# A hybrid decoder layer with product-key experts: the second half's output product and norm in one pass of four blocks

## The chip, the cores and the metric

The kernel runs on one core of a Trainium2 chip. Its time is the device time of one execution in microseconds (us), and the median of several executions is compared. Five engines work side by side, each through its own queue of instructions: TensorE (PE, matrix products), VectorE (DVE), ScalarE (ACT), GpSimd (POOL) and SyncE (SP, which issues most DMA transfers). Semaphores order the engines among each other.

## The reference

One step of a one-layer decoder: 1024 prompt tokens and 8 sample tokens of width 1024. Three gated branches (dilated attention, a convolution, attention to a memory) are merged; what concerns this change comes after the merge:

```python
x1 = x + merged @ w_o
h2 = rms_norm(x1, g_norm2)
y  = x1 + peer(h2)

def peer(xb):                                   # for each token
    q = (xb @ w_pq).reshape(nb, 8, 2, 128)      # 8 heads, two halves of a key
    s = einsum('bhcd,ckd->bhck', q, sub_keys)   # 2 x 128 scores a head
    s1, i1 = top_k(s[:, :, 0], 16); s2, i2 = top_k(s[:, :, 1], 16)
    sc, ci = top_k(s1[..., :, None] + s2[..., None, :], 16)
    e = i1[ci // 16] * 128 + i2[ci % 16]        # 128 experts a token, of 16384
    g = softmax(sc)
    return einsum('be,bed->bd', g * gelu(xb . u_tab[e]), v_tab[e])
```

## The kernel before

All products are made in float32 precision from split operands: a weight or activation is cast to a shorter float on ACT (L158, L170), the residue is formed on DVE (L159, L171), and `mm3` (L173 to L176) issues three matmuls for one product. `load_w` (L161) loads 128 x 1024 values of a weight (512 KB) and splits them.

The 1024 prompt tokens are eight blocks of 128. The kernel goes through the first half (blocks 0 to 3, with the sample tokens as a fifth block) and then through the second (4 to 7). For a half, `front` makes the branches and the merged rows, and `tail` (L759) does the rest: the product with `w_o` into PSUM banks `po` (L775 to L789, eight `load_w` calls), the sum `x1`, its store to `x1scr`, the norm with `g_norm2` (`norm_rows`), the store of `h2` to `h2scr`, and its transposed split copy `h2h`, `h2l`. Then `topk` (L809) makes the queries (`pq`, 16 column groups of `w_pq`), the scores, and on DVE the selection: the best 16 of 128 twice (L847 to L851), the best 16 of their sums (`cand`, L862 to L876), one-hot lookups (L903 to L913), and the indices (`idxB`, L942, one of the last steps of a block that goes to the gathers).

The experts are worked off in two ways. Blocks 0 to 4 go the **dense** way: `gate_build` (L1016) makes gate matrices of all 16384 experts (products `pG`, stored to `gscr`), and `peer_dense` (L1063) goes over the expert table in 128 chunks `i1` of 128 experts: `pa` = scores of 640 tokens in two halves, gelu on ACT into `ge` (L1102), times the gate `Gt` on DVE (L1104), split into `hh` (L1107) and `hl` (L1108), and after each six chunks the products `pv` with `v_tab`, in two column halves, added into `dacc` (L1124). `uh`, `ul` are the split of a chunk of `u_tab`, `vh`, `vl` of `v_tab`. Chunks go through two `ge` buffers and three score banks. Blocks 5 to 7 go by **gathers**: `peer_gather` (L961) fetches for each of 128 slots a row of `u_tab` and `v_tab` for every token by an indirect DMA on POOL (L981), forms the dot product on DVE (L985) and adds the weighted row into `gacc` (L995). Half of the gather buffers (`uv0_2`, `uv0_3` and on) and the dense accumulator `dacc` lie in memory that the selection of the second half uses until its last step.

Before, the second half's tail runs twice: `tail("1a")` for blocks 4 and 5, with the gate build of block 4 behind it, and `tail("1b")` for blocks 6 and 7. In both, three PSUM banks serve the `po` and `pq` products.

A list scheduler fixes the order of each engine's queue when the kernel is built, from the priorities that stand in the code (`tc.cur_priority`); the gathers are given a lower priority than the work around them. On the chip a queue is worked off in that order.

Of the kernel before, what the change touches and what calls it, by code (L numbers as in the profile page):

```python
# [10 lines left out]
F32R = mybir.dt.float32r  # L11
# [10 lines left out]
P = 128  # L22
D = 1024
KD = D // P
# [22 lines left out]
def peer_trunk(tc, I, O):  # L47
# [11 lines left out]
    with contextlib.ExitStack() as es:  # L59
# [699 lines left out]
        def tail(tid, keep, wp, merged_h, merged_l, tblocks, after=None, kpool=None):  # L759
# [4 lines left out]
            with contextlib.ExitStack() as left:  # L764
                left.enter_context(banks(f"tail{tid}"))
                hp = left.enter_context(tc.tile_pool(name=f"h2t{tid}", bufs=1))
                with tc.tile_pool(name=f"tail{tid}", bufs=1) as tp:
# [7 lines left out]
                    for cg in range(2):  # L775
                        gs = slice(cg * 512, cg * 512 + 512)
                        pss = [mm_tile(f"po{tid}{cg}{c0}") for c0, _, _ in tblocks]
                        for kk in range(4):
                            wh, wl = load_w(wp, w_o[:, 2 * kk : 2 * kk + 2, gs], 2, 512, f"o{tid}{cg}{kk}")
                            for j in range(2):  # L780
                                k = 2 * kk + j
                                for bi, (c0, n, _) in enumerate(tblocks):
                                    sl = slice(c0, c0 + n)
                                    mm3(
                                        pss[bi][:n], merged_h[:, k, sl], merged_l[:, k, sl], wh[:, j], wl[:, j],
                                        k == 0, k == KD - 1,
                                    )
                        for bi, (c0, n, _) in enumerate(tblocks):
                            nc.vector.tensor_tensor(x1[bi][:n, gs], x1[bi][:n, gs], pss[bi][:n], op=OP.add)  # L789
                    if tid == "0":  # L790
                        h2h = keep.tile([P, KD, HALF + NS], F32R, tag="hTh", name=f"h2h{tid}")
                        h2l = keep.tile([P, KD, HALF + NS], F32R, tag="hTl", name=f"h2l{tid}")
                    else:
                        h2h = hp.tile([P, KD, TT], F32R, name=f"h2h{tid}")
                        h2l = hp.tile([P, KD, TT], F32R, name=f"h2l{tid}")
# [6 lines left out]
                with contextlib.ExitStack() as kes:  # L802
                    kp = kpool or kes.enter_context(tc.tile_pool(name="topk", bufs=1, side="right"))
                    topk(tid, kp, wp, h2h, h2l, [(c - m0, n, row) for c, n, row in tblocks], left, after)

        def topk(tid, kp, wp, h2h, h2l, tblocks, left, after):
            TT = sum(n for _, n, _ in tblocks)
            tchunks = [(0, TT)] if TT <= 512 else [(0, TT // 2), (TT // 2, TT // 2)]
            nb = len(tblocks)  # L809
            sv = kp.tile([P, nb, 16, TOPK], F32, name=f"sv{tid}")  # L810
            ix = kp.tile([P, nb, 16, TOPK], U32, name=f"ix{tid}")
            wx = left.enter_context(tc.tile_pool(name=f"wx{tid}", bufs=1)) if tid == "1a" else wp
            for hc in range(16):
# [3 lines left out]
                for c0, cn in tchunks:  # L817
                    cs = slice(c0, c0 + cn)
                    pq = mm_tile(f"pq{tid}{hc}{c0}")
                    for k in range(KD):  # L820
                        mm3(pq[:, :cn], wh[:, k], wl[:, k], h2h[:, k, cs], h2l[:, k, cs], k == 0, k == KD - 1)
# [306 lines left out]
        with tc.tile_pool(name="keep", bufs=1) as keep, tc.tile_pool(name="wts", bufs=1) as wp:  # L1128
# [3 lines left out]
            tail("0", keep, wp, *mg, [(b * P, P, b * P) for b in range(4)] + [(HALF, NS, SEQ)])  # L1132
            tc.cur_priority = p0
            phase.update(mm=3, o=1, g=2)
            with tc.tile_pool(name="psG", bufs=1, space=PSUM) as pgs:
# [11 lines left out]
                with (  # L1147
# [5 lines left out]
                    tail(  # L1153
                        "1a", keep, wp, *mg, [(b * P, P, HALF + b * P) for b in (0, 1)],
                        after=lambda b: gate_build(gb, pgs, (b * P, b * P + P), 8), kpool=kp,
                    )
                    tail("1b", keep, wp, *mg, [(b * P, P, HALF + b * P) for b in (2, 3)], kpool=kp)
# [88 lines left out]
```

## Time and profile before

| | |
|---|---|
| median of 3 runs | 3703.09 us (3703.05 to 3704.65) |
| profiled execution | 3695.24 us |
| its span | 3693.1 us |
| PE busy | 3429.9 us, 93% |
| DVE busy | 2899.1 us, 78% |
| ACT busy | 1499.6 us, 41% |
| POOL busy | 565.7 us, 15% |

The rows come from one profiled execution, whose own time stands beside its span. In a row of a window, "PE busy (x)" is the time in which the engine worked and how many instructions; PEld is the load of weights into PE; PEclk is the clock granted to PE as a share of full speed; then follow the mean busy share of the 16 DMA engines and what they moved. In a timeline a row begins with the start and the duration of an instruction (x3: three in a row), and what stands in brackets is the idle time before it and what ended it. A row of waits gives microseconds in total, their number, and the longest.

The stages along the span: memory and first front to about 655 us, first `w_o` pass and queries to 843, first selection to about 1007, gate build of blocks 0 to 3 with the second front to 1555, then the second half's tail to about 1897 with the dense pass beginning at 1828, and dense pass and gathers to the end.

### The profile page before, as it was taken

The page shows a single profiled execution, that of the slowest core. Times are in us where ns is not written, and L with a number is a line of the kernel's source. Part 1 is how long each engine was busy: PE and PEld are TensorE (multiplying, and loading weights), DVE is VectorE, ACT ScalarE, POOL GpSimd, SP SyncE. Part 2 cuts the span into 40 slices and gives each one's busy share as a digit, 9 for nine tenths or more (in the row PEclk, how much of TensorE's full clock was granted, in tenths as well). Part 3 has the DMA queues.
Part 4 walks back from the last instruction along what each step waited for, and adds up shares of the span by engine and source line. Part 5 has one row for each costly group of instructions (what it writes and reads, how often), then busy time and mean ns, then how long its engine had stood idle before and what let it go on. Part 6 is the DMA issues. An engine that isn't in the chain of part 4 may idle for free.

```text
span 3693.1 us, 55182 instructions
## 1 busy us (share of the span) xinstructions
PE 3429.9 (93%) x19969; PEld 3011.5 (82%) x19969; DVE 2899.1 (78%) x6275; ACT 1499.6 (41%) x3519; POOL 565.7 (15%) x398
## 2 busy tenths in 40 slices
PE   8987999898889989887899999999999999999998
PEld 6766989697677778676798888888989888898987
DVE  4358555499998656779988888887988888798988
ACT  6553552235755554344443333332333333233332
POOL 0000000000000000000012323322323332233332
PEclk9997999999999999998799999999999999999999
DMA  5467455423355546753668988888988988888987
GB/s 180 136 199 259 154 184 183 154 86 119 103 186 189 177 157 211 246 188 131 224 233 314 338 312 330 310 318 309 336 328 324 342 315 304 308 327 318 334 329 279
DMA packets 338454, 902.09 MB, mean 244 GB/s; under 512 B 32588, under 2 KB 140276, under 8 KB 285436
## 3 DMA queue, kind: packets, MB, share of 16 engines
q1 hardware_dynamic: 281732, 487.49, 39.7%
q0 software_dynamic: 56448, 411.07, 29.2%
q8 instruction: 157, 2.57, 0.3%
q14 instruction: 117, 0.96, 0.1%
HBM read 804.09 MB, written 94.83 MB: 243 GB/s over the span
## 4 chain that ended last, share of the span: by engine, by line
PE 31%; issue 30%; DVE 14%; DMA 13%; POOL 11%; ACT 2%; SPq 0%; POOLq 0%; DVEq 0%; ACTq 0%
POOL uv L981 11%; DMA uv<-in_uv,idxB 4%; PE pg L175 2%; PE pg L174 2%; PE pg L176 2%; PE pG L1057 2%; PE pG L1056 2%; DMA vr<-in_v_tab 1%; PE p_q L175 1%; PE p_q L176 1%; DMA wko<-kscr 1%; PE p_q L174 1%; DMA uv<-in_uv,idxS 1%; PE pa L174 1%; PE pa L176 1%
## 5 line engine op out<-in xcount | busy, mean ns | idle before, releaser
L981 POOL DMA_INDIRECT uv<-in_uv,idxB x384 | 555.8, 1448 | 1553.2 <-DVE gacc L995 1226.1
L174 PE MATMUL pa<-h2Ah,uh 128*128 128x320 f32 x2048 | 633.7, 310 | 2.2 <-ACT uh L158 2.2
L176 PE MATMUL pa<-h2Ah,ul 128*128 128x320 f32 x2048 | 631.9, 310 | 2.3 <-DVE ul L159 2.2
L175 PE MATMUL pa<-h2Al,uh 128*128 128x320 f32 x2048 | 633.2, 309 | 0.0
L985 DVE CUSTOM_DVE_ANT_0 uv<-uv,gh 128x1024 f32<-128x1024 f32 x392 | 478.5, 1222 | 138.2 <-DMA uv<-in_uv,idxB 119.9
L174 PE MATMUL pv<-vh,hh 128*128 128x512 f32 x1280 | 480.5, 396 | 44.3 <-ACT vh L158 28.4
L995 DVE SCALAR_TENSOR_TENSOR gacc<-uv,av,gacc 128x1024 f32<-128x1024 f32 x392 | 502.5, 1282 | 17.5 <-ACT av L993 12.6
L175 PE MATMUL pv<-vl,hh 128*128 128x512 f32 x1280 | 505.2, 395 | 9.3 <-DVE vl L159 9.3
L176 PE MATMUL pv<-vh,hl 128*128 128x512 f32 x1280 | 499.9, 393 | 0.0
L174 PEld LDWEIGHTS pa<-h2Ah,uh 128*128 128x128 f32 x2048 | 385.7, 188 | 6.9 <-ACT uh L158 2.4
L176 PEld LDWEIGHTS pa<-h2Ah,ul 128*128 128x128 f32 x2048 | 385.1, 188 | 5.4 <-DVE ul L159 2.8
L175 PEld LDWEIGHTS pa<-h2Al,uh 128*128 128x128 f32 x2048 | 385.4, 188 | 3.3 <-issue 0.9
L158 ACT CAST vh<-vr 128x512 fp32r<-128x512 f32 x256 | 157.2, 619 | 422.0 <-DMA vr<-in_v_tab 238.1
L174 PEld LDWEIGHTS pv<-vh,hh 128*128 128x128 f32 x1280 | 242.7, 190 | 99.0 <-ACT vh L158 40.0
L175 PEld LDWEIGHTS pv<-vl,hh 128*128 128x128 f32 x1280 | 243.6, 190 | 61.0 <-DVE vl L159 12.9
L176 PEld LDWEIGHTS pv<-vh,hl 128*128 128x128 f32 x1280 | 243.4, 190 | 50.0
L981 POOL DMA_INDIRECT uv<-in_uv,idxS x8 | 9.2, 1149 | 1556.3 <-ACT co L739 1513.2
L159 DVE TENSOR_TENSOR vl<-vr,vh 128x512 fp32r<-128x512 f32 x256 | 175.6, 688 | 77.0 <-ACT vh L158 76.5
L174 PE MATMUL pg<-hTh,wh_g 128*128 128x260 f32 (+1 forms) x576 | 192.9, 335 | 0.0
L175 PE MATMUL pg<-hTl,wh_g 128*128 128x260 f32 (+1 forms) x576 | 192.4, 334 | 0.0
L176 PE MATMUL pg<-hTh,wl_g 128*128 128x260 f32 (+1 forms) x576 | 192.3, 334 | 0.0
L990 ACT ACTIVATE av<-av 128x2 f32<-128x2 f32 x196 | 39.9, 204 | 375.3 <-DVE av L985 374.8
(558 smaller groups left out, 7651.3 us busy)
## 6 DMA issues: line engine op xcount, KB each, us to landing
ur<-in_uT SPq DMA_DIRECT2D x128, 512.0 KB
vr<-in_v_tab SPq DMA_DIRECT2D x256, 256.0 KB
gscr<-stg SPq DMA_DIRECT2D x20, 2048.0 KB
Gt<-gscr SPq DMA_DIRECT2D x32, 1280.0 KB
wr_g<-in_w_col SPq DMA_DIRECT2D x48, 512.0 KB
wr_q<-in_w_in SPq DMA_DIRECT2D x24, 512.0 KB
wr_u<-in_w_col SPq DMA_DIRECT2D x16, 512.0 KB
wr_pq<-in_w_col SPq DMA_DIRECT2D x16, 512.0 KB
```

The lines of the kernel that those rows point to most:

```text
L158: nc.scalar.copy(hi, raw)
L159: nc.vector.tensor_tensor(lo, raw, hi.bitcast(F32), op=OP.subtract)
L174: nc.tensor.matmul(out, ah, bh, start=start, stop=False)
L175: nc.tensor.matmul(out, ah, bl, start=False, stop=False)
L176: nc.tensor.matmul(out, al, bh, start=False, stop=stop)
L981: nc.gpsimd.indirect_dma_start(out=uv, out_offset=None, in_=I["uv"], in_offset=bass.IndirectOffsetOnAxis(ap=col, axis=0),)
L985: nc.vector.tensor_tensor_reduce(out=uv[:, 0:D], in0=uv[:, 0:D], in1=h2, scale=1.0, scalar=0.0, op0=OP.mult, op1=OP.add, accum_out=av[:, s ...
L990: nc.scalar.activation(av, av, AF.Gelu_apprx_tanh)
L995: nc.vector.scalar_tensor_tensor(acc, uv[:, D:], av[:, j : j + 1], acc, op0=OP.mult, op1=OP.add)
L1056: nc.tensor.matmul(pG[:, q], o2[:, a, :, q], wh[:, a, :, q], start=True, stop=False)
L1057: nc.tensor.matmul(pG[:, q], o2[:, a, :, q], wl[:, a, :, q], start=False, stop=True)
```

## The change

`tail` is called once for the second half, with all four blocks. The `po` product of the fourth block takes a bank of the transposes (`t_tile` slot 2), since there are three `mm` banks. `h2h` and `h2l` lie for both halves in `keep`, where they stood for the first half only. `topk` is called by a function that `tail` is given: for the second half twice, "1a" for blocks 4 and 5 (with the gate build of block 4 behind it) and "1b" for blocks 6 and 7. The product with `w_pq` reads its columns with the offset `m0`. So `w_o` is loaded, cast and split eight times for the second half instead of sixteen, and `g_norm2` once instead of twice.

```diff
-        def tail(tid, keep, wp, merged_h, merged_l, tblocks, after=None, kpool=None):
+        def tail(tid, keep, wp, merged_h, merged_l, tblocks, choose):
...
-                hp = left.enter_context(tc.tile_pool(name=f"h2t{tid}", bufs=1))
...
-                        pss = [mm_tile(f"po{tid}{cg}{c0}") for c0, _, _ in tblocks]
+                        pss = [
+                            mm_tile(f"po{tid}{cg}{c0}") if bi < phase["mm"] else t_tile(f"po{tid}{cg}{c0}", 2)
+                            for bi, (c0, _, _) in enumerate(tblocks)
+                        ]
...
-                    if tid == "0":
-                        h2h = keep.tile([P, KD, HALF + NS], F32R, tag="hTh", name=f"h2h{tid}")
-                        h2l = keep.tile([P, KD, HALF + NS], F32R, tag="hTl", name=f"h2l{tid}")
-                    else:
-                        h2h = hp.tile([P, KD, TT], F32R, name=f"h2h{tid}")
-                        h2l = hp.tile([P, KD, TT], F32R, name=f"h2l{tid}")
+                    h2h = keep.tile([P, KD, HALF + NS], F32R, tag="hTh", name=f"h2h{tid}")
+                    h2l = keep.tile([P, KD, HALF + NS], F32R, tag="hTl", name=f"h2l{tid}")
...
-                with contextlib.ExitStack() as kes:
-                    kp = kpool or kes.enter_context(tc.tile_pool(name="topk", bufs=1, side="right"))
-                    topk(tid, kp, wp, h2h, h2l, [(c - m0, n, row) for c, n, row in tblocks], left, after)
-
-        def topk(tid, kp, wp, h2h, h2l, tblocks, left, after):
+                choose(h2h, h2l)
+
+        def topk(tid, kp, wp, h2h, h2l, tblocks, after=None):
...
+            left = contextlib.ExitStack()
...
-                        mm3(pq[:, :cn], wh[:, k], wl[:, k], h2h[:, k, cs], h2l[:, k, cs], k == 0, k == KD - 1)
+                        ms = slice(m0 + c0, m0 + c0 + cn)
+                        mm3(pq[:, :cn], wh[:, k], wl[:, k], h2h[:, k, ms], h2l[:, k, ms], k == 0, k == KD - 1)
...
-                    tail(
-                        "1a", keep, wp, *mg, [(b * P, P, HALF + b * P) for b in (0, 1)],
-                        after=lambda b: gate_build(gb, pgs, (b * P, b * P + P), 8), kpool=kp,
-                    )
-                    tail("1b", keep, wp, *mg, [(b * P, P, HALF + b * P) for b in (2, 3)], kpool=kp)
+                    blocks1 = [(b * P, P, HALF + b * P) for b in range(4)]
+
+                    def choose1(h2h, h2l):
+                        topk("1a", kp, wp, h2h, h2l, blocks1[:2], lambda b: gate_build(gb, pgs, (b * P, b * P + P), 8))
+                        topk("1b", kp, wp, h2h, h2l, blocks1[2:])
+
+                    tail("1", keep, wp, *mg, blocks1, choose1)
```

The scheduler's order changes with it. The first place is DVE at the start of the dense pass. Names that end in `1b0` and `1b1` belong to the selection of blocks 6 and 7, `ge0`, `hl0` to chunk 0 of the dense pass, `ul3` to chunk 3, `uv0_2` to slot 2 of the first gathered block. Before, from the first gate product on:

```order
L873 MAX_INDEX pu1b1_19080<-sc161b1_19079,cand1b1_19076 128x8
L1104 TENSOR_TENSOR ge0_21611<-ge0_21611,Gt0_21603 128x640
L873 MAX_INDEX pu1b1_19080<-sc161b1_19079,cand1b1_19076 128x8
L159 TENSOR_TENSOR ul3_21800<-ur3_21797,uh3_21798 128x1024
L873 MAX_INDEX pu1b1_19080<-sc161b1_19079,cand1b1_19076 128x8
L946 TENSOR_TENSOR gB_132<-gt1b0_19066,gsm1b0_19069 128x128
L1104 TENSOR_TENSOR ge1_21675<-ge1_21675,Gt0_21603 128x640
```

The gate products of chunks 0 and 1 stand among the steps of the selection. Its end comes 89 rows behind `ge0`:

```order
L913 TENSOR_TENSOR iq11b1_19162<-oh11b1_19155 128x128
L942 SCALAR_TENSOR_TENSOR idxB_131<-iq01b1_19152,iq11b1_19162 128x128
L1124 TENSOR_TENSOR dacc_21597<-dacc_21597,pv000_21991 128x512
L1124 TENSOR_TENSOR dacc_21597<-dacc_21597,pv001_21992 128x512
L159 TENSOR_TENSOR ul8_22396<-ur8_22393,uh8_22394 128x1024
L1104 TENSOR_TENSOR ge6_22269<-ge6_22269,Gt4_21861 128x640
L985 ISA uv0_2_19198,av0_2_19197<-uv0_2_19198,gh20_19181 128x1024
```

The dot of `uv0_2` stands behind the gate product of chunk 6 (`ge6`). After, the end of the selection:

```order
L911 TENSOR_TENSOR oh11b1_19082<-oh11b1_19082 128x128x2
L913 TENSOR_TENSOR iq11b1_19089<-oh11b1_19082 128x128
L942 SCALAR_TENSOR_TENSOR idxB_131<-iq01b1_19079,iq11b1_19089 128x128
L985 ISA uv0_2_19126,av0_2_19125<-uv0_2_19126,gh20_19109 128x1024
L985 ISA av0_2_19125 128x1
L985 ISA uv0_4_19138,av0_4_19137<-uv0_4_19138,gh20_19109 128x1024
```

Here the gathers' dots follow the last index at once. From the fourth of them on to chunk 0:

```order
L985 ISA uv0_3_19129,av0_2_19125<-uv0_3_19129,gh20_19109 128x1024
L985 ISA av0_2_19125 128x1
L995 SCALAR_TENSOR_TENSOR gacc0_19110<-uv0_2_19126,av0_2_19125,gacc0_19110 128x1024
L995 SCALAR_TENSOR_TENSOR gacc0_19110<-uv0_3_19129,av0_2_19125,gacc0_19110 128x1024
L995 SCALAR_TENSOR_TENSOR gacc0_19110<-uv0_4_19138,av0_4_19137,gacc0_19110 128x1024
L159 TENSOR_TENSOR ul4_21794<-ur4_21791,uh4_21792 128x1024
L995 SCALAR_TENSOR_TENSOR gacc0_19110<-uv0_5_19141,av0_4_19137,gacc0_19110 128x1024
L1104 TENSOR_TENSOR ge0_21539<-ge0_21539,Gt0_21531 128x640
L1104 TENSOR_TENSOR ge1_21603<-ge1_21603,Gt0_21531 128x640
L1108 TENSOR_TENSOR hl0_21594<-ge0_21539,hh0_21593 128x640
```

So the whole selection and the first four gathers' dots and sums now stand ahead of `ge0`.

The second place is SP's queue at the same point: `Gt0`, `Gt4` are the gate loads of chunks 0 to 7, `dacc` the five loads of the dense accumulator, `vr00` the first rows of `v_tab`, `stg608` the last gates of block 4. Before:

```order
L1061 DMA gscr_126<-stg608_17748 128x4096
L1092 DMA ur3_21797<-in_uT 128x1024
L1089 DMA Gt0_21603<-gscr_126 128x20x128
L1089 DMA Gt4_21861<-gscr_126 128x20x128
L1116 DMA vr00_21996<-in_v_tab 128x512
L1092 DMA ur4_21863<-in_uT 128x1024
```

After:

```order
L1061 DMA gscr_126<-stg544_17673 128x4096
L1061 DMA gscr_126<-stg576_17783 128x4096
L1061 DMA gscr_126<-stg608_17893 128x4096
L1077 DMA dacc_21525<-x1scr_124 128x1024 x5
L1089 DMA Gt0_21531<-gscr_126 128x20x128
L1089 DMA Gt4_21789<-gscr_126 128x20x128
L1116 DMA vr00_21924<-in_v_tab 128x512
```

The loads of `dacc`, which before came some 20 rows behind `vr00`, now stand ahead of `Gt0`.

## Rows read from the trace of the kernel before

**Rows 1.** The page: busy time, share of the span, instructions.
```profile
PE 3429.9 (93%) x19969; PEld 3011.5 (82%) x19969; DVE 2899.1 (78%) x6275; ACT 1499.6 (41%) x3519; POOL 565.7 (15%) x398
```

**Rows 2.** Windows: length; PE, PEld, DVE, ACT, POOL busy; PEclk, DMA share, GB/s.
```profile
1558.85:1630.00 71.15, 54.60 (x307) 46.84 (x306) 44.76 (x103) 27.70 (x46) 2.88 (x2) 0.87 0.65 230
1630.00:1846.00 216.00, 175.76 (x1208) 161.44 (x1207) 215.89 (x862) 97.13 (x159) 6.10 (x4) 0.87 0.50 172
1846.00:1897.00 51.00, 51.00 (x300) 47.42 (x299) 48.45 (x133) 28.29 (x37) 0.00 (x0) 1.00 0.56 174
```

**Rows 3.** The window of the dense pass, same columns.
```profile
1860.00:3694.00 1834.00, 1771.16 (x9802) 1603.64 (x9800) 1552.87 (x2062) 586.80 (x1330) 549.74 (x380) 0.99 0.86 316
```

**Rows 4.** Waits of PE, 1860 to 3694: us in total, times, longest.
```profile
PE pv L174 <- ACT vh L158: 28.4, 11, 5.4
PE pv L174 <- DVE dacc L1124: 12.9, 4, 7.4
PE pv L175 <- DVE vl L159: 9.3, 8, 4.1
```

**Rows 5.** Timeline of DVE, 1847 to 1908: start, us, instruction, idle before.
```profile
1847.65 0.83 DVE L1104 TENSOR_TENSOR ge<-ge,Gt 128x640 f32<-128x640 f32 x1 [1.27 <-DMA Gt<-gscr]
...
1896.70 0.29 DVE L942 SCALAR_TENSOR_TENSOR idxB<-iq01b,iq11b 128x128 int32<-128x128 f32 x1
...
1906.83 1.23 DVE L985 CUSTOM_DVE_ANT_0 uv<-uv,gh 128x1024 f32<-128x1024 f32 x1 [2.36 <-DMA uv<-in_uv,idxB]
```

**Rows 6.** Timeline of PE: the first `pv`.
```profile
1855.60 1.32 PE L174 MATMUL pv<-vh,hh 128*128 128x512 f32 x5
```

**Rows 7.** Groups by form on DVE, 1846 to 1897: busy us, mean ns.
```profile
L159 DVE TENSOR_TENSOR vl<-vr,vh 128x512 fp32r<-128x512 f32 x9 | 6.2, 685 | 0.0
L159 DVE TENSOR_TENSOR ul<-ur,uh 128x1024 fp32r<-128x1024 f32 x5 | 6.1, 1226 | 0.0
L1104 DVE TENSOR_TENSOR ge<-ge,Gt 128x640 f32<-128x640 f32 x6 | 5.0, 829 | 1.3 <-DMA Gt<-gscr 1.3
L1108 DVE TENSOR_TENSOR hl<-ge,hh 128x640 fp32r<-128x640 f32 x6 | 4.9, 823 | 1.0 <-ACT hh L1107 1.0
```

**Rows 8.** Timeline of PE: the first and the last `w_o` matmuls of blocks 4, 5.
```profile
1554.99 0.47 PE L174 MATMUL po1a<-wh_o1a,mgh 128*128 128x512 f32 x1 [2.75 <-ACT mgh L752]
...
1588.98 0.39 PE L175 MATMUL po1a<-wl_o1a,mgh 128*128 128x512 f32 x1
1589.21 0.40 PE L176 MATMUL po1a<-wh_o1a,mgl 128*128 128x512 f32 x1
```

**Rows 9.** Waits of DVE, 1558.85 to 1650.
```profile
DVE wl_pq1a L159 <- ACT wh_pq1a L158: 11.6, 6, 7.2
DVE wl_o1a L159 <- ACT wh_o1a L158: 7.5, 3, 4.3
```

**Rows 10.** Timelines of POOL and SP: gather, accumulator and gate loads issued.
```profile
1897.79 0.94 POOL L981 DMA_INDIRECT uv<-in_uv,idxB  x1 [105.86 <-PE pa L176]
...
1897.02 2.30 SPq L1077 DMA_DIRECT2D dacc<-x1scr  x5
...
1839.67 3.40 SPq L1089 DMA_DIRECT2D Gt<-gscr  x2
```

**Rows 11.** Timeline of DVE: the first gathers' dots and sums.
```profile
1907.98 1.22 DVE L985 CUSTOM_DVE_ANT_0 uv<-uv,gh 128x1024 f32<-128x1024 f32 x1
...
1915.09 4.00 DVE L995 SCALAR_TENSOR_TENSOR gacc<-uv,av,gacc 128x1024 f32<-128x1024 f32 x3
1919.00 0.82 DVE L1108 TENSOR_TENSOR hl<-ge,hh 128x640 fp32r<-128x640 f32 x1
```

**Rows 12.** A window in which PE waits often, columns as in rows 2.
```profile
1800.00:1820.00 20.00, 12.79 (x91) 11.10 (x89) 20.00 (x76) 8.72 (x17) 0.00 (x0) 0.59 0.60 226
```

**Rows 13.** Timeline of PE at the end: its two waits.
```profile
3673.88 0.50 PE L174 MATMUL pv<-vh,hh 128*128 128x512 f32 x1 [2.79 <-ACT hh L1107]
...
3679.93 0.50 PE L174 MATMUL pv<-vh,hh 128*128 128x512 f32 x1 [2.37 <-DVE dacc L1124]
```

## What the change was predicted to do

> **What bounds the kernel now.** I read the page first: TensorE (PE) is busy 93% of the span [rows 1]. A share over the span does not say what an edit in one place is worth, so next come the windows of the only stretch that the change touches, from the last merged block to the start of the dense expert pass [rows 2]. Three things are to be seen there. From 1558.85 to 1630 us nobody is full: PE 54.60 and VectorE (DVE) 44.76 of 71.15 us. From 1630 to 1846 DVE is busy 215.89 of 216.00 us and PE 175.76: this is the selection and the gate build, and DVE sets its pace. From 1846 to 1897 both are full at once, PE 51.00 of 51.00 and DVE 48.45: PE is in the dense pass while DVE still finishes the selection of blocks 6 and 7. Then the dense pass itself, from 1860 on: PE 1771.16 of 1834 us, DVE 1552.87 [rows 3]. It is bound by PE; its three largest named waits sum to 28.4 + 12.9 + 9.3 = 50.6 us [rows 4]. So a microsecond by which the dense pass starts later or earlier is a microsecond at the end, unless those 50.6 us take it up. The whole question is when the dense pass gets going.
>
> Its start is read from DVE's timeline [rows 5]: the first gate product, ge of chunk 0 (L1104), is at 1847.65, and only 49 us later, at 1896.70, comes the last index of the selection (L942). PE began its first pv, the product that needs ge's results, at 1855.60 and without a wait [rows 6]. The chunk loop has three score banks and two ge buffers, so PE can compute scores up to the first half of chunk 3, and then needs chunk 0 to be through hl (L1108) to go on.
>
> **What the change removes.** Eight loads of w_o of 512 KB, eight ACT casts and eight DVE subtracts. ACT was busy 97.13 of 216 us and the DMA engines half of the time [rows 2], so casts and loads are hidden there and I cost them at nothing. The subtracts are of the shape of ul, 1.23 us [rows 7], of which neighbours overlap some 0.1: 8 x 1.13 = 9.0 us of DVE. The number of matmuls is the same. One g_norm2 load goes too; nothing in the rows waits for it.
>
> **What it moves: PE.** The pass over w_o now has 192 matmuls in a row instead of 96 twice. They follow each other by 0.23 us (1588.98 to 1589.21); the first half's 96 took from 1554.99 to 1589.6 [rows 8], 34.6 us, of which 96 x 0.23 = 22 us are matmuls and 12 holes. The 96 more, 22 us, can fill the holes: the pass ends 10 us later than the first half did, and DVE, which has only the subtracts and adds in it, idles up to 10 us more.
>
> **What it moves: DVE, the term that decides.** DVE's two orders differ at one place: before, ge and hl of chunks 0 to 5 stand between the steps of the last selection; after, every step of that selection stands first, then four gather dots, two weight residues and four gather sums, and then ge of chunk 0. DVE works its queue off as it stands, so the dense pass must wait for all of that. How late is it?
> Work on DVE from 1558.85 to the last index, before: 44.76 + 215.89 + 48.45 = 309.1 us [rows 2]. Off it come 9.0 us of subtracts and the dense work that now stands behind the index, six ge, six hl, five ul, nine vl [rows 7]: 5.0 + 4.9 + 6.1 + 6.2 = 22.2 us of busy time, and less some 0.09 of overlap for each of the 26, 20 us. Left are 280 us.
> DVE's idle time before was 71.15 - 44.76 = 26.4 us in the first window and 0.1 and 2.6 in the others, 29.1 in all. Its largest causes were the weight casts, 11.6 and 7.5 us [rows 9]. After, the longer w_o pass adds up to 10, while four norms in a row close some of the old gaps. Bounds: 27 us (the pass costs nothing) and 44 us (it adds 10, and the query weights come 5 late behind the norm's stores); I take 34, nearer the row of before.
> Last index after: 1558.85 + 280 + 34 = 1873 us (1866 to 1883), against 1896.70. So far the change gains 24 us, on the gathers' side.
> Now the rest of the queue. The first of the four dots needs memory that is free only after the last index: before, GpSimd (POOL) issued that gather at 1897.79 [rows 10], and DVE ran its dot at 1906.83 [rows 5], 10.1 us after the index. SyncE (SP) stands in the same line: its five loads of the dense accumulator went out at 1897.02 and took 2.30 us to issue, and in the new order the two Gt loads of 1280 KB and the first v rows are queued behind them, while before Gt had gone out at 1839.67 [rows 10]. So the landing gets 2.6 MB more to share with; at 316 GB/s, the mean of the dense pass [rows 3], that is 8 us at most, and nothing if the gathers go first: 10 to 18, I take 11, near the row. Then four dots at 1.15 (1906.83 to 1907.98), two ul at 1.13 and four sums at 1.30 (three from 1915.09 to 1919.00) [rows 11]: 4.6 + 2.3 + 5.2 = 12 us. ge of chunk 0 then starts at 1873 + 11 + 12 = 1896, 48 us later than before. PE gets on once ge, the cast hh, hl and the next gelu are through, some 3 us at 0.8 or less each [rows 7]: 1899. Before, it went on at 1855.60. PE is late by **43 us**.
>
> The Trainium skill ("Perfetto Trace Analysis", Optimization Strategy) speaks against such an edit: where the busiest engine changes over time, it advises to interleave the regimes, and this takes them apart. The window in which both engines were full agrees with it; it gives a sign and no size. For the landing, the skill's ceiling of the 16 DMA engines, 435 GB/s ("DMA: Bandwidth & Descriptors", Where 436 GB/s comes from), would make an estimate of 6 us in place of the 8; no row here bears it out for this landing.
>
> **Two small terms.** While PE waits its clock falls: in 1800 to 1820, where it was busy 12.79 of 20 us, the granted clock was 0.59 [rows 12], in 1846 to 1897, without a gap, 1.00 [rows 2]. Coming out of a wait of some 20 us it will run a little at the low level; between nothing and 5 us lost, I take 2. At the end, before shows PE waiting 2.79 us for hh and 2.37 for dacc at 3673.88 and 3679.93 [rows 13], where the last gathers' sums stand in DVE's queue between the dense steps. After, the gathers are some 13 ahead at each chunk and are over before the last pv, so this and some of the last group may go: between nothing and 8, I take 4. Sum: 43 + 2 - 4 = **+41 us**. The profiled execution took 3695.24 us; against its own time the sum makes 3736. The median is 3703.09, 7.85 above it; carried there, **3744 us**.
>
> **Rivals.**
> (A) The other side: not slower. The dense pass takes the delay back. The gathers start 24 us earlier and run ahead, so their dots no longer hold up vl, hl and dacc, and the vr loads meet less traffic late: if all 50.6 us of PE's waits and the tail's 4 went, 3703 + 43 + 2 - 51 - 4 = 3693 us. It decides from some 45 us on. For it: the DMA share is 0.86 in the dense pass [rows 3], and the largest wait, 28.4 us for vh [rows 4], follows late loads. Against it: the number of gathers to a chunk is the same in both orders all the way, about three, so the traffic in the middle is the same and only the last few chunks are free of it. Half of it gone gives 3720. Chance of the full effect 0.09.
> (B) The change does only what it says: DVE saves 9.0 us, the selection's move is hidden, the dense pass starts 9 us earlier: 3694 us. This needs ge to run before the index; even with no idle at all on DVE, ge comes at 1558.85 + 280 + 12 = 1851, no earlier than the 1847.65 of before. Chance 0.03.
> (C) It costs more: the w_o and query passes run at the lower clock because PE has holes in them, so that DVE's idle is 44 us or above, the Gt loads land late behind the accumulator, and chunks 4 to 8 wait for ur and vr that are queued behind both. 10 + 7 + 3 + 5 more give 3769. Chance 0.15.
> My forecast's own case: 0.73.
>
> **How the numbers follow.** The likeliest is 3744 us. Its unknowns are idle on DVE (-7, +10), the landing (-1, +7), the clock (-2, +3), the tail (-4, +4): taken together some -14 and +16, so 3730 to 3760. The range reaches down past the half of (A) and up to most of (C): 3717 to 3765. What a measurement can tell from no change is about 0.2%, 7.4 us. Slower needs above 3710.5: the forecast, (C) and nothing of the full (A), 0.88. The full (A) and (B), 0.12, end within that bound or under 3695.7; as they stand at its edge, 0.07 and 0.05.
>
> **What the profile after would show.** Right: the last idxB at 1866 to 1883, ge of chunk 0 behind four gather sums at 1889 to 1905, a PE wait of 15 us or more on ge, hl or ul just before it, full clock lost there, and a dense pass as long as before within 10 us. Wrong: if ge starts before 1870 the order did not bind; if the dense pass from the first pv on is over 20 us shorter, (A) was at work; if the last idxB is after 1890, the w_o pass cost DVE more than I gave it.

## The result, and the profile after

The changed kernel takes 3753.38 us (median of 4 executions, 3738.88 to 3758.93), the kernel before 3703.07 (4 executions, 3691.36 to 3704.65). The ratio is 1.0122, with a 95% interval of 1.0094 to 1.0150: slower. A second set on another chip gave 1.0130 (1.0104 to 1.0155). The forecast was 3744 us, in a range of 3717 to 3765. The profiled execution took 3738.88 us with a span of 3737.1, that is 44.0 more than the span of before.

PE's busy time has hardly moved, as the page shows (busy us, share of the span, instructions; before: [rows 1]):

```profile
PE 3431.0 (92%) x19969; PEld 3016.3 (81%) x19969; DVE 2896.4 (78%) x6267; ACT 1487.7 (40%) x3507; POOL 577.1 (15%) x398
```

So 43 of the 44 us are time in which PE stands idle; its busy time is only 1.1 us longer. The windows of the changed stretch tell where (columns as in [rows 2]; the last row answers to [rows 3]):

```profile
1558.85:1630.00 71.15, 61.64 (x301) 51.33 (x300) 45.25 (x82) 26.28 (x45) 2.88 (x2) 0.90 0.71 259
1630.00:1846.00 216.00, 148.53 (x1090) 139.20 (x1089) 210.92 (x935) 83.81 (x139) 3.93 (x4) 0.81 0.36 122
1846.00:1875.00 29.00, 11.73 (x86) 9.43 (x83) 26.18 (x50) 12.13 (x16) 1.22 (x2) 0.50 0.37 149
1875.00:1905.00 30.00, 23.59 (x124) 23.33 (x125) 16.71 (x20) 7.94 (x18) 5.83 (x5) 0.74 1.04 368
1905.00:3738.00 1833.00, 1773.35 (x9794) 1607.35 (x9792) 1525.47 (x1985) 581.21 (x1320) 555.46 (x374) 0.98 0.85 312
```

Up to 1630 PE does 7 us more than before, since the pass over `w_o` is in one piece. From 1630 to 1846 it does 27 us less, while DVE is nearly as full as before (210.92 us against 215.89). From 1846 to 1875, where it ran without a gap before, it is busy 11.73 of 29 us, at a granted clock of 0.50, the low level. The dense pass from 1905 on is as busy as before.

DVE's timeline at the dense pass's start, in answer to [rows 5]:

```profile
1872.39 0.29 DVE L942 SCALAR_TENSOR_TENSOR idxB<-iq01b,iq11b 128x128 int32<-128x128 f32 x1
...
1882.37 1.22 DVE L985 CUSTOM_DVE_ANT_0 uv<-uv,gh 128x1024 f32<-128x1024 f32 x1 [9.69 <-DMA uv<-in_uv,idxB]
...
1893.83 1.31 DVE L995 SCALAR_TENSOR_TENSOR gacc<-uv,av,gacc 128x1024 f32<-128x1024 f32 x1
1895.07 1.55 DVE L1104 TENSOR_TENSOR ge<-ge,Gt 128x640 f32<-128x640 f32 x2
```

The last index comes 24.3 us earlier than before, the first gate product 47.4 us later. PE's timeline shows where it goes on: behind the gelu of chunk 2, at 1898.02.

```profile
1866.14 0.29 PE L1057 MATMUL pG<-oh,oh 128*128 128x128 f16 x1
...
1875.27 0.64 PE L174 MATMUL pa<-h2Ah,uh 128*128 128x320 f32 x1 [8.83 <-ACT ge L1102]
...
1898.02 0.64 PE L174 MATMUL pa<-h2Ah,uh 128*128 128x320 f32 x1 [6.15 <-ACT ge L1102]
```

All this would do as a confirmation. But the first of these rows, the last product of block 4's gate build, is one that the prediction did not look at. Before, it stands at 1830.38:

```profile
1830.38 0.29 PE L1057 MATMUL pG<-oh,oh 128*128 128x128 f16 x1
```

The gate build ends 36 us later than before. It begins as much later. Its first one-hots on DVE, after and then before:

```profile
1765.82 0.66 DVE L1047 TENSOR_TENSOR oh<-iotaT,ig 128x1024 f16<-128x1024 f16 x1
```

```profile
1727.33 0.70 DVE L1047 TENSOR_TENSOR oh<-iotaT,ig 128x1024 f16<-128x1024 f16 x1
```

The build itself takes about as long as it did (98.7 us from the first one-hot to the end of the last, 101.0 before). What stands ahead of it on DVE is the selection of blocks 6 and 7: of its 64 index searches (`ix1b`) 52 come before the first one-hot, before the change 4.

The waits of PE from the last merged block on name the reason: the products wait for DVE's one-hots (`oh`, L1049 and L1051). After:

```profile
PE pG L1057 <- DVE oh L1051: 23.1, 10, 4.9
PE pG L1056 <- DVE oh L1049: 11.1, 6, 3.3
```

and before:

```profile
PE pG L1057 <- DVE oh L1051: 6.6, 5, 2.4
PE pG L1056 <- DVE oh L1049: 1.4, 1, 1.4
```

and SP's timeline shows the last gates stored late and the gate loads behind them and behind `dacc` (compare [rows 10]; the first row is the stores of the last gates, in which SP stands 38 us):

```profile
1829.41 38.00 SPq L1061 DMA_DIRECT2D gscr<-stg  x3
...
1873.46 2.34 SPq L1077 DMA_DIRECT2D dacc<-x1scr  x5
1875.84 13.71 SPq L1089 DMA_DIRECT2D Gt<-gscr  x2
```

The first gelu, whose buffer lies in the memory of the last gates, has to wait for their store. On ACT, after:

```profile
1873.48 1.28 ACT L1102 ACT_TABLE_LOAD   x1 [6.41 <-DMA gscr<-stg]
```

and before:

```profile
1839.71 0.44 ACT L1102 ACTIVATE ge<-pa 128x320 f32<-128x320 f32 x1 [0.59 <-DMA gscr<-stg]
```

So three things are late at the same place: DVE's queue reaches `ge` at 1895.07, the gate loads finish issuing at 1889.55, and the gates that they load are stored only at 1873. The experiments ask which of them makes the time.

### The profile page after: what moved, and what is told of

It is laid out like the page before. It is cut to its first block, busy times and chain, and to the rows that moved or that the text cites. A ratio compares the mean times of both kernels' runs of the same rounds, so it can differ in the third digit from the quotient of the medians.

```text
span 3737.1 us, 55139 instructions
## 1 busy us (share of the span) xinstructions
PE 3431.0 (92%) x19969; PEld 3016.3 (81%) x19969; DVE 2896.4 (78%) x6267; ACT 1487.7 (40%) x3507; POOL 577.1 (15%) x398
## 4 chain that ended last, share of the span: by engine, by line
PE 43%; issue 20%; DVE 15%; DMA 12%; POOL 7%; ACT 2%; SPq 1%; POOLq 0%; ACTq 0%; DVEq 0%
POOL uv L981 7%; PE pv L174 3%; PE pv L175 3%; PE pv L176 3%; DMA uv<-in_uv,idxB 3%; PE pa L176 3%; PE pa L174 3%; PE pa L175 3%; PE pg L175 2%; PE pg L176 2%; PE pg L174 2%; DMA vr<-in_v_tab 2%; DMA ur<-in_uT 2%; PE pG L1057 1%; PE pG L1056 1%
## 5 line engine op out<-in xcount | busy, mean ns | idle before, releaser
L981 POOL DMA_INDIRECT uv<-in_uv,idxB x384 | 566.4, 1475 | 1535.7 <-DVE gacc L995 1217.6
L174 PE MATMUL pa<-h2Ah,uh 128*128 128x320 f32 x2048 | 638.7, 312 | 15.9 <-ACT ge L1102 15.7
L158 ACT CAST uh<-ur 128x1024 fp32r<-128x1024 f32 x128 | 134.3, 1049 | 174.5 <-PE pa L175 131.2
```

Of the source, the lines that this page charges most:

```text
L158: nc.scalar.copy(hi, raw)
L174: nc.tensor.matmul(out, ah, bh, start=start, stop=False)
L981: nc.gpsimd.indirect_dma_start(out=uv, out_offset=None, in_=I["uv"], in_offset=bass.IndirectOffsetOnAxis(ap=col, axis=0),)
```

## The experiments

Runs differ by up to 11 us in the stage ahead of the change. There all the kernels have the same instructions in the same order, until the loads and casts of `w_o` begin, shortly before the anchor. So the profiles are compared from one anchor, the start of the last `mgl` on DVE (L753, 1558.24 before). All numbers in the table are us behind that anchor, read from the timelines as above: last gate product of block 4 (`pG`), first `ge` product (L1104), last `idxB`, end of the span. The last column is the ratio of the times to the kernel before, from all timed executions.

| kernel | `pG` | `ge` | `idxB` | end | ratio (95%) |
|---|---|---|---|---|---|
| before | 272.1 | 289.4 | 338.5 | 2134.9 | 1 |
| changed | 305.3 | 334.2 | 311.6 | 2176.3 | 1.0122 (1.0094 to 1.0150) |
| changed, again (e9) | 304.2 | 333.2 | 310.5 | 2176.3 | 1.0130 (1.0104 to 1.0155) |
| e1: gate load first | 305.3 | 327.5 | 311.5 | 2178.0 | 1.0107 (1.0084 to 1.0130) |
| e12: e1 again | 305.5 | 327.0 | 311.8 | 2169.5 | 1.0122 (1.0098 to 1.0146) |
| e10: dots behind | 304.8 | 331.7 | 311.0 | 2186.6 | 1.0143 (1.0118 to 1.0168) |
| e11: e10 with e1 | 305.5 | 326.5 | 311.8 | 2172.8 | 1.0123 (1.0099 to 1.0147) |
| e2: gates first | 223.6 | 302.9 | 345.9 | 2170.5 | 1.0073 (1.0056 to 1.0091) |
| e3: sums after gates | 277.8 | 319.0 | 345.2 | 2160.4 | 1.0035 (1.0020 to 1.0049) |
| e4: order without saving | 329.5 | 358.9 | 335.8 | 2207.2 | 1.0214 (1.0195 to 1.0234) |
| e5: paced by gates | 279.0 | 297.7 | 331.4 | 2151.6 | 1.0036 (1.0013 to 1.0058) |
| e6: gates even | 257.8 | 299.9 | 328.0 | 2155.3 | 1.0100 (1.0062 to 1.0139) |
| e7: gates ahead | 249.2 | 293.7 | 331.4 | 2157.0 | 1.0061 (1.0038 to 1.0083) |
| e8: paced, no saving | 300.6 | 319.8 | 353.7 | 2169.3 | 1.0076 (1.0046 to 1.0106) |

**The queue ahead of `ge`: e1, e10, e11, e12.** First the loads of the accumulator were moved behind the gate loads on SP.

```diff
                 acc = da.tile([P, NB, D], F32, name="dacc")
+                pacc = tc.cur_priority
+                tc.cur_priority = pacc + 1500
                 for b in range(NB):
                     nc.sync.dma_start(acc[:, b], x1scr[b * P : (b + 1) * P, :])
+                tc.cur_priority = pacc
```

> The changed kernel, with the five loads of the dense accumulator put behind the first gate loads (priority + 1500), so that SP issues Gt0 and Gt4 ahead of dacc. In DVE's order ge of chunk 0 moves ahead of one ul and four gather sums; the whole selection and four gather dots still stand before it. Theory (DVE's queue decides): ge of chunk 0 comes 5.2 + 1.1 = 6 us earlier, at about 1889 in place of 1895, and the time is about 6 us below the changed kernel's (ratio to before about 1.0105 in place of 1.0122). Rival 1 (SP decides, Gt behind dacc: Gt's issue took 13.7 us from 1875.84): the gain is 10 us or more. Rival 2 (neither, the late gate build decides): no gain.

`ge` came 6.7 us earlier, as the theory said. It starts without a wait, right behind a residue and the dots, so in e1 DVE's queue decides, as its theory has it (DVE's timeline in e1):

```profile
1885.68 1.55 DVE L1107 TENSOR_TENSOR ge<-ge,Gt 128x640 f32<-128x640 f32 x2
```

Whether that reaches the end is not settled: on the first chip the ratio is 0.0015 lower than the changed kernel's elsewhere, and on one chip with it (e9 and e12) 0.0008, well inside both intervals.

> The changed kernel itself, once more, on the chip on which the next three run, so that they can be compared with it and not only with the kernel before. Ratio to before 1.009 to 1.015; from the last mgl on DVE, the last index at 312 us and ge of chunk 0 at 334.

> e1 again on the chip of e9, with more rounds: Gt ahead of dacc alone. ge of chunk 0 at 327.5 as in e1, 6.7 us before the changed kernel; if that reaches the end, the ratio is 0.0018 below e9's.

The changed kernel repeated itself: last index at 310.5, `ge` at 333.2. So did e1, at 327.0.

Then the direct test of the prediction's term: the four dots and sums were put behind `ge` of chunks 0 and 1. For this the call of `peer_gather` stands behind that of `peer_dense`, with its priority kept; `pG` and the last index stay where they were (304.8 and 311.0).

```diff
+                    if begun is not None and blkid == 0 and s0 == G:
+                        nc.scalar.activation(h2, h2, AF.Copy, scale=begun)
...
+                        if i1 == 0:
+                            begun = small.tile([P, 1], F32, tag="begun", bufs=1, name="begun")
+                            nc.vector.tensor_scalar(begun, ge[:, 0:1], 0.0, 1.0, op0=OP.mult, op1=OP.add)
...
-        peer_gather(gp, [gp, gp2], range(NGB))
...
-        peer_dense()
+        begun = peer_dense()
+        tc.cur_priority = gprio
+        peer_gather(gp, [gp, gp2], range(NGB), begun)
```

> The changed kernel, but the row of h2 that the gathers' dots read is multiplied, on ACT and before slot 2 of the first gathered block, by a one that DVE writes from ge of chunk 0. So the four dots and four sums now stand behind ge and hl of chunks 0 and 1; the selection is still ahead of them, and SP still issues the accumulator's loads ahead of Gt. Theory A (as predicted: DVE's queue, 11 + 12 us of it the dots' landing and work): ge of chunk 0 comes 20 us earlier, at 314. Theory B (Gt, queued on SP behind dacc, was about as late, its issue having ended at 328.7 in the changed kernel): ge at 328 to 333, gain under 6 us, ratio as e9 within 0.002.

> e10 and e1 together: dots behind ge of chunk 0, and Gt issued ahead of dacc. Theory A: ge of chunk 0 at 314 or a little later. Theory B (Gt follows the storing of the last gates, 312.6, and lands some 8 us later as in the kernel before, where ge came 8.0 us after Gt's issue): ge at 320 to 322, 13 us before the changed kernel, ratio 0.003 to 0.004 below e9. What then still separates it from before (289) is the late gate build, 33 us.

Theory A fell. With the dots gone from ahead of it, `ge` gained 1.5 us against e9 and not 20, and the row says what it waits for now (DVE's timeline in e10):

```profile
1894.43 1.56 DVE L1106 TENSOR_TENSOR ge<-ge,Gt 128x640 f32<-128x640 f32 x2 [2.90 <-DMA Gt<-gscr]
```

With Gt first as well (e11), it still waits for Gt, 5 us earlier from the anchor:

```profile
1890.96 1.56 DVE L1109 TENSOR_TENSOR ge<-ge,Gt 128x640 f32<-128x640 f32 x2 [3.94 <-DMA Gt<-gscr]
```

This is 326.5 us behind the anchor, 4.5 us above Theory B's 320 to 322, and no better than e1 and e12, which leave the dots where they are. Its ratio is 0.0007 below e9's, not the 0.003 to 0.004 expected, and well inside the intervals. So the queue of dots and the gate load end within a few microseconds of each other, and taking away one shows the other. Both together are worth about 7 of the 45 us. Of the remaining 37, 33 are there at the last gate product: upstream, where the gate build and the selection share DVE.

**The order of gate build and selection: e2, e3, e5, e6, e7.** In all five the four-block pass stays, and the edit aims at DVE's order alone. In e2 the tile of the best 16 of blocks 6 and 7 lies in memory of the gate build, so that their selection cannot start before it is over; in e3 only the candidate sums are held back in this way.

```diff
+                        with tc.tile_pool(name="gb1", bufs=1, side="right") as gb:
+                            topk("1a", kp, wp, h2h, h2l, blocks1[:2], lambda b: gate_build(gb, pgs, (b * P, b * P + P), 8))
+                        with tc.tile_pool(name="late1b", bufs=1, side="right") as lp:
+                            topk("1b", kp, wp, h2h, h2l, blocks1[2:], None, lp)
...
+            sv = (lp or kp).tile([P, nb, 16, TOPK], F32, name=f"sv{tid}")
```

(e3 has the last line for `cand` in place of `sv`.)

> The changed kernel, with the four-block pass kept, but with the best-16 tile of blocks 6 and 7 in memory of the gate build's pool, so that their selection can start only when block 4's gate build is over. In DVE's order ge of chunk 0 again stands amid the selection (75 rows before the last index, before: 89). Theory (the order decides, not the pass): ge of chunk 0 at 1838 to 1850, last index at about 1890, time 9 us below to 3 us above before: 3694 to 3706, ratio 0.9975 to 1.001. Rival (the four-block pass itself costs, by PE's lower clock and DVE's idle time): ratio stays above 1.008.

> As e2, but only the sums of the candidates (the last third of the selection of blocks 6 and 7) wait for the gate build; the 16 best-16 steps still run between the gate build's one-hots. ge of chunk 0 stands 37 rows before the last index. Theory: PE gets its first gelu only when block 4's gates are stored (1873 in the changed kernel, about 1862 here with some 10 us of sums moved behind), so the dense pass starts 10 to 20 us later than before: ratio 1.003 to 1.006. Rival (only the index and the gathers' dots ahead of ge cost, 22 us, and the gate build is no limit): ratio 1.000 or below.

e2 landed between theory and rival. `ge` came back from 334.2 to 302.9, which the order explains, but not as far as the 1838 to 1850 that I expected: it stands at 1869.18, and its last index at 1912.21 in place of 1890. DVE now stands idle. It has 45.1 us of idle time up to the last index, against 30.8 in the changed kernel, 9.5 of them in one wait for the gates' store, through the shared memory, as DVE's waits show (1650 to 1869):

```profile
DVE sv1b L847 <- DMA gscr<-stg: 9.5, 1, 9.5
```

e3 has the ratio that was expected, for another reason: the gate build ended at 277.8 already, but the loads of Gt need the memory in which the candidates lie, and were issued only at 1877.14. SP's issue waits for the searches in these candidates (`pu1b`, L876), and `ge` for the loads:

```profile
1884.80 1.56 DVE L1104 TENSOR_TENSOR ge<-ge,Gt 128x640 f32<-128x640 f32 x2 [1.58 <-DMA Gt<-gscr]
```

Both use memory to hold work back, and memory brings waits of its own. So the next three hold it back by data: each of the 16 gate steps leaves a one, by which ACT scales the scores that a best-16 step reads.

```diff
+                        mk = marks[min(16, hc - 4)] if marks and hc - 4 > 0 else None
+                        if mk is not None:
+                            nc.scalar.activation(
+                                sc[:, b0 : b0 + full].rearrange("p a b -> p (a b)"), pSs[:, : full * P], AF.Copy, scale=mk
+                            )
...
                     nc.vector.tensor_tensor(wl, o1, cols(3), op=OP.mult)
+                    if marks is not None:
+                        mk = marks[0].tile([P, 1], F32, name=f"mk{t0}_{tb}")
+                        nc.vector.tensor_scalar(mk, wl[:, 0, 0, 0:1], 0.0, 1.0, op0=OP.mult, op1=OP.add)
+                        marks.append(mk)
```

(e6 and e7 have `hc + 1` and `hc + 5`.)

> The changed kernel with the four-block pass kept and the order paced by data: each of block 4's 16 gate steps writes a one (128 x 1) from its last DVE result, and the copy of the scores of blocks 6 and 7 (ACT, before each of the 16 best-16 steps) is scaled by the one of gate step hc - 4. So the selection can run at most about four steps ahead of the gate build. ge of chunk 0 then stands 59 rows before the last index (changed kernel: 15 behind it, before: 89 ahead). Measured from the last mgl on DVE, before had ge of chunk 0 at 289 us and the changed kernel at 334. Theory (order of the gate build against the selection, and the queue ahead of ge, carry the loss, the pass itself gains): ge of chunk 0 at 285 to 300, last index at 320 to 335, ratio to before 0.996 to 1.003. Rival (the four-block pass costs by PE's clock and idle time, whatever the order): ratio above 1.007 as in e2.

> As e5, with the one of gate step hc + 1: a selection step may start only when the gate build is a step ahead. Theory: gates a little earlier, the last index a little later, ge of chunk 0 53 rows before it: about as e5, within 0.2%, ratio 0.997 to 1.004; if DVE then waits for query products, some 5 to 10 us more, towards e2 (1.0073).

> As e5, with the one of gate step hc + 5. ge of chunk 0 stands 68 rows before the last index. Theory: between e6 and e2, since DVE idles while the query products of blocks 6 and 7 wait for their turn: ratio 1.000 to 1.006, and the idle time shows on DVE between 1660 and 1850 us. Rival (the earlier the gates, the earlier the dense pass): below e5.

e5 is the clearest: the same work as the changed kernel plus 16 tiny DVE instructions, with no more idle time on DVE to speak of (32.1 us up to the last index, 30.8 in the changed kernel), and `pG` is back from 305.3 to 279.0, `ge` from 334.2 to 297.7, the end from 2176.3 to 2151.6, the ratio from 1.0122 to 1.0036. The rows, last gate product on PE:

```profile
1844.32 0.30 PE L1067 MATMUL pG<-oh,oh 128*128 128x128 f16 x1
```

and first `ge` on DVE:

```profile
1863.02 0.83 DVE L1114 TENSOR_TENSOR ge<-ge,Gt 128x640 f32<-128x640 f32 x1 [1.41 <-DMA Gt<-gscr]
```

The first one-hot of the gate build stands at 184.0 behind the anchor (205.0 in the changed kernel, 169.1 before), with 20 index searches of blocks 6 and 7 ahead of it. So DVE's order carries 36 of the 45 us at `ge`, and most of the loss at the end. This one edit moves both chains, since `ge` also comes ahead of the last index again: 26 of the 36 us are there at the last gate product, and 10 come behind it.

The expectation's ratio, 0.996 to 1.003, was a little too good all the same, and e6 and e7 did not come out as I thought. Their gates end earlier still (257.8, 249.2), their `ge` comes at 299.9 and 293.7, and yet neither is faster than e5: e6 is above it, at 1.0100, and e7, at 1.0061, cannot be told from it, since the intervals overlap. The idle time on DVE that e7's expectation named is not there either: up to the last index it has 32.1 us, as e5.

What the rest is made of can be divided, though not explained. A fixed point for PE is the matmul from which 9820 are left, the first `pv` of before [rows 6]; what is left from there on is the same work in before, the changed kernel, e5 and e6, and all but a few matmuls in e7. Us behind the anchor at which PE reaches it, and us from there to the end:

| kernel | reaches it | to the end |
|---|---|---|
| before | 297.4 | 1837.5 |
| changed | 337.2 | 1839.1 |
| e5 | 307.4 | 1844.2 |
| e6 | 312.3 | 1843.1 |
| e7 | 307.1 | 1850.0 |
| e1 | 331.0 | 1847.0 |
| e12 | 330.7 | 1838.9 |

So PE still goes on 10 us late in e5 and e7, and the dense pass is 7 and 12 us longer. But e1 and e12 are one and the same kernel, and differ by 8 us there, so most of the second part may be no more than what varies from one execution to the next. One of its waits is that for `vh`, 45.5 us in e7 against 28.4 in [rows 4]:

```profile
PE pv L174 <- ACT vh L158: 45.5, 8, 11.0
```

This wait varies between profiles without a pattern that the runs explain (21.7 in the changed kernel, 31.1 in its repetition, 62.9 in e3), and stays open. No version was found that beats the kernel before.

**What sharing the loads is worth: e4, e8.** Both load, cast and split `w_o` twice for the second half, e4 in the changed kernel's order, e8 in e5's.

```diff
-                    for cg in range(2):
...
+                    for b0, part in ([(0, tblocks)] if tid == "0" else [(0, tblocks[:2]), (2, tblocks[2:])]):
+                        for cg in range(2):
```

> The changed kernel, but with w_o loaded, cast and split twice for the second half, for blocks 4, 5 and then for 6, 7; the norms, the queries and the selection follow for all four blocks as in the changed kernel, and DVE's and SP's orders at the start of the dense pass are the changed kernel's. Theory: the order alone carries the loss; the eight subtracts are worth at most 9.0 us and fall partly into DVE's idle time there: 3 to 9 us above the changed kernel, ratio to before 1.013 to 1.015. Rival (the pass of 192 matmuls in a row is what costs): the loss goes, ratio below 1.006.

> e5 with w_o loaded, cast and split twice for the second half; DVE's order is that of e5 with eight rows more. It prices the sharing alone in an order in which the dense pass isn't behind the selection. Theory 1 (only the subtracts count): 9 us above e5. Theory 2 (as e4 against the changed kernel: casts and holes of a second pass count too): 20 to 26 us above e5.

The expectation of e4 fell, and so did its rival, that the pass of 192 matmuls in a row is what costs. `ge` and the last index come 24.7 and 24.2 us later than in the changed kernel (e4), and 22.1 and 22.3 later than in e5 (e8). That is the size of e8's Theory 2. In time it is less plain: e4's ratio is 0.0092 above the changed kernel's, measured on another chip, some 34 us, and e8 is 13 us above e5 (3729.14 and 3716.18), between the two theories, with intervals that overlap a little. Up to the last index DVE has 9.7 us more work in e4, the subtracts, and 14.6 more idle time (45.4 against 30.8). Most of that is its waits for the casts of `w_o` (1550 to 1700). They are, in e4,

```profile
DVE wl_o L159 <- ACT wh_o L158: 20.1, 9, 9.0
```

and in the changed kernel

```profile
DVE wl_o L159 <- ACT wh_o L158: 8.0, 3, 4.2
```

which is 12 us. In the kernel before, the second pass over `w_o` stood among the best-16 steps of blocks 4 and 5 and DVE did not wait for it at all: its group of eight subtracts has no idle time before it (page of groups, busy us, mean ns, idle before):

```profile
L159 DVE TENSOR_TENSOR wl_o1b<-wr_o1b,wh_o1b 128x1024 fp32r<-128x1024 f32 x8 | 10.0, 1253 | 0.0
```

So in these runs the second pass was dear where nothing hid it. Before, its casts were hidden; that removing it there gives the 9 us of subtracts and no more is an estimate from that row, and no run shows it alone.

## Why the prediction came out right

The path that it summed was there, and nearly every term has its size; that this path is the whole cause was wrong. Step by step, from the profile of the changed kernel:

- **DVE's work and idle time up to the last index.** Predicted 280 us of work and 34 of idle time (27 to 44), last index at 1873. Measured, from the last `mgl`: 280.8 and 30.8, last index at 1872.39. The 9.0 us for the subtracts and the 20 for the dense work that changed sides are borne out by this sum.
- **The pass over `w_o`.** Predicted to end 10 us later than the first half's did, with up to 10 us more of idle time on DVE, taken as 5. It ends at 1599.5 against 1589.6, and DVE's idle time, counted from the anchor, went from 29.0 to 30.8. This also settles rival (C), which needed 44 or above.
- **The gathers' landing.** Predicted 11 us behind the last index (10 to 18); 10.0.
- **Dots, residues, sums ahead of `ge`.** Predicted 12 us; 12.7, from 1882.37 to 1895.07.
- **PE goes on.** Predicted at 1899; 1898.02. That is 42.4 behind the 1855.60 of before; predicted 43.
- **The small terms.** Predicted +2 for the clock and -4 for the tail. The clock did fall: 0.50 in the window from 1846 to 1875, 0.74 in the next. From the point where PE goes on, 1855.60 before and 1898.02 after, the same 9820 matmuls are left, and they take 1837.5 us before and 1839.1 after: 1.6 more, where the two terms together had 2 less. The difference is less than the 8 us by which e1 and e12 differ there, so it does not say which of the two is off.
- **The sum.** +41 on the profiled execution; 43.6 measured, 41.4 from the anchor. The median came out 9 above the forecast of 3744: the other three executions took 3751 to 3759, at granted clocks of 0.948 to 0.950 where the profiled one had 0.953. Where that clock was lost in them no profile shows.
- **The range.** It was built from parts of -7, -1, -2, -4 below and +10, +7, +3, +4 above, "some -14 and +16". The lower side is their plain sum; the upper would then be +24, so that "3730 to 3760" is narrower above than its own parts. The measured median lies inside it either way.
- **The sign on PE.** A wait of 15 us or more on `ge`, `hl` or `ul` just ahead of `ge` was named. PE's waits for the gelu sum to 15.7 us, in three pieces of 8.8 us at most, and those for `ul` to 7.9; the longest is the one for the gates' store, which the forecast did not have.

**Rival (A)**, that the dense pass takes the delay back, is refuted. From the same matmul on, the dense pass is 1.6 us longer and not some 50 shorter. PE's idle time between `ge` and the end is 61.7 us, before 61.9. The named waits changed places, they did not go (1558.85 to the end; compare [rows 4]):

```profile
PE pv L174 <- DVE dacc L1124: 22.8, 5, 8.5
PE pv L174 <- ACT vh L158: 21.7, 9, 5.2
...
PE pv L175 <- DVE vl L159: 3.0, 5, 1.1
```

**Rival (B)** needed `ge` ahead of the last index; it stands 22.7 us behind it.

**What was wrong inside the right number.** The step "DVE works its queue off as it stands, so the dense pass must wait for all of that" is true, and the sum along that queue gave `ge` to a microsecond. But the prediction took it for the only chain, and so for the cause. e10 takes the dots out of that chain and gains 1.5 us at `ge` and nothing in time. There was a second chain: the one-hots of block 4's gates fall back behind the best-16 steps of blocks 6 and 7, since those are ready earlier (their first index search stands 124.0 us behind the anchor, before 164.4); so the last gates are stored at 1873 in place of 1839, and their load, queued behind `dacc` and sharing the DMA engines with it and with the gathers (DMA share 1.04 from 1875 to 1905), lands when DVE gets to `ge`. What the prediction says of SP, that the Gt loads are queued behind the accumulator's, was seen, but priced as traffic in the way of the gathers' landing and not as a chain of its own. Of the 45 us at `ge`, 33 are there when the last gate product ends (305.3 against 272.1), and 12 come behind it, of which e1, e11 and e12 take back about 7. The forecast of an end did not suffer from this, since both chains end together: in e10 the gate load lets `ge` start 2.5 us before the changed kernel's. A forecast of a repair would have suffered: moving the dots, which the prediction's reading suggests, gives nothing that the times show. That the second chain did not end later than the first was luck, since no term of the sum stood for it.

The Trainium skill's advice ("Perfetto Trace Analysis", Optimization Strategy) is that interleaving regimes with different busiest engines may help. The runs agree: e5, which differs from the changed kernel in the order and 16 tiny instructions, has the ratio 1.0036 in place of 1.0122.

## What to carry to other kernels

When work is made ready earlier, ask whose place in a full engine's queue it takes: here the selection of two blocks, ready sooner by a shared pass, went ahead of one-hots for which the busiest engine was waiting. A sum along one queue that ends at the right time does not show that this queue is the cause; look for every chain that ends at the same instruction (the operand's load, the buffer's last reader, the queue) before calling it so, and take one away to test it. And price a saving where it stands: sharing eight loads took 22 to 25 us off the start of the dense pass where nothing hid the second pass, and an estimated 9 us where its casts had been hidden.

## What the runs showed of the hardware

The stage ahead of the change, with the same instructions in the same order but for the first steps on `w_o`, took between 1558.1 and 1569.2 us to the same instruction in the fourteen profiles, a spread as large as the effects of single edits. Comparing profiles from an anchor at the start of the changed stretch took this out: the changed kernel and its repetition then agree to 1.1 us at `pG`, `ge` and `idxB`, and end at 2176.3 both. The repeated e1 and e12 agree to 0.5 us at `ge`, but end 8.5 us apart (2178.0 and 2169.5): an anchor takes out what varies ahead of it, and not what varies behind.
